# Columns of g2 summed late: one half among the last pieces of the output projection, the other between the first experts' weights

## The chip, the cores and the metric

The kernel runs on one core of a Trainium2 chip. The metric is the device time of one execution in microseconds. Engines are called PE (TensorE: matmuls, with its weight loads as PEld), DVE (VectorE), ACT (ScalarE), POOL (GpSimd) and SP (SyncE, which here only issues transfers).

## What is computed

One layer of a decoder trunk on 256 tokens of width 2048, in float32: a mixer of four kinds of attention with one input and one output projection, then a mixture of 16 experts. A vector c of the sequence gives six vectors by which the layer is modulated; g2, the last, scales the experts' output, column by column.

```python
mod = c_act @ ada_w[l] + ada_b[l]                      # c_act = silu(c); ada_w is 2048 x 12288
sh1, sc1, g1, sh2, sc2, g2 = jnp.split(mod, 6, axis=-1)
h = rmsnorm(x, norm1_g[l]) * (1.0 + sc1[:, None]) + sh1[:, None]
x = x + g1[:, None] * token_mixer(h, w_in[l], ..., w_out[l])
h = rmsnorm(x, norm2_g[l]) * (1.0 + sc2[:, None]) + sh2[:, None]
x = x + g2[:, None] * moe_ffn(h, router_w, router_bias, exp_w_gate[l], exp_w_up[l], exp_w_down[l])
return rmsnorm(x, final_g)
```

The reference computes all 16 experts for all tokens with a weight that is zero but for two; the kernel gathers, for each expert, up to 64 tokens (CAP) that chose it.

## The kernel before

**Stages.** Up to 146 us the sums for sc1 and sh1 run with the first pieces of the input projection; from 146 to 435 us the rest of the input projection, with the attention of the four mixers in between; then the output projection, to 547 us; the routing, to 557 us; then the experts in 8 pairs, and the last norm.

**The weight stream.** All weights come through one list of units in a fixed order, which SP issues (the class `Stream`). A unit is 128 partitions x 1024 float32 columns, 512 KB; a gate or up weight is a double unit of 1 MB (128x2048). Units wait in slots: a ring of 11 (names r, r_94 to r_98), and slots that are added when other data has been used up (ug, uo, uw, usc, ush among them; ugu is the name of a gate/up weight in such a slot, udh of a down weight). A slot takes its next unit when its last one has been read (`stream.done`); a unit can't pass the units ahead of it in the list. Two kinds of slot, for g2r and yhl, are used once and are added when all units ahead of the experts' have been issued.

**Projections.** A piece of w_in or w_out is one unit. `halves` splits it into a high part on ACT (whi, L584) and a low part on DVE (wlo, L586), in two buffers each (SPLITS = 2); then 24 matmuls read them (L561 to L563 with the weights moving or L565 to L567, names acc for the input and oacc for the output projection). In the output projection there are 32 pieces; each time that 512 columns of the result are complete, `add_part` multiplies them by g1 and adds them to x (L1190 and L1191 on DVE).

**The columns of the modulation.** g1 comes by matmuls, in 512-wide units between the pieces of the output projection (`akeys2`, from a list TAIL, at most 1.2 times the piece's number plus AHEAD). sc2, sh2 and g2 come on DVE: each in two blocks of 1024 columns, each block of 16 units. `ada_acc_v` multiplies the first unit by an element of c for each partition (L509) and adds the others in the same way, one operation for each (L511), to a running sum (ada_v). When a block is complete, `ada_cols` takes four matmuls with ones and a transpose (L520 to L523) to make columns of it (g2c). The units of the three stand among the pieces of the input projection (`akeys`, 96 units, evenly). `finish_cols` starts the last step of blocks whose sum is done.

**g2 as a row.** The experts' output has tokens in partitions, so g2 is needed as a row in all of them (g2r). `spread` makes 512 columns of it: four times a diagonal matrix of a column (dg, L533, DVE) and a matmul with ones (ada_r, L534), then a copy on ACT (L535). Before, the four calls stand in the loop over the first pair's eight weights, at n = 4 to 7. The first reader of g2r is the output of the first down projection (L1537).

**The routing.** After the last logits: a sum of squares (L1292), a root in steps of which one is on ACT (L1293, L405 to L414), the logits (L1305), then the choice of experts and the places of their tokens (to L1345).

**The experts.** For each pair p, `pair_units` lists 16 gate/up units (GUORDER: (c, g) for c = 0, 1, then 2 and 3, each for two experts) and 16 down units. The first pair's loop gathers the tokens (pg, L1410) as it goes, multiplies (gatep, upp, L201 and L204), and releases each weight behind its last matmul. The order on each engine is the order in which the program is recorded, changed by a scheduler that moves instructions forward where their operands allow.

Of the kernel before, what the change touches and what calls it, by code (L numbers as in the profile page):

```python
# [11 lines left out]
F32 = mybir.dt.float32  # L12
# [15 lines left out]
VEC = {(n, h) for n in ("sc2", "sh2", "g2") for h in range(2)}  # L28
TAIL = ("g1",)
NEG = -1e30  # L30
# [150 lines left out]
def hybrid_trunk_kernel(  # L181
# [59 lines left out]
    def wout_units(n):  # L241
# [10 lines left out]
        return [((("o", n), u), mk(u)) for u in range(8)]  # L252

    def pair_units(p):
        def mkg(c, g, e):
            return lambda t: nc.sync.dma_start(t, (gateT, upT)[g][:, c, 2 * p + e])
# [8 lines left out]
        def mkc(c):  # L265
            return lambda t: nc.sync.dma_start(
                t.rearrange("p (e f n) -> p e f n", e=2, f=4),
                downT[:, 2 * p:2 * p + 2, :, 1536 + 128 * c:1664 + 128 * c])
        us = [((("gu", p), c, g, e), mkg(c, g, e), 2) for c, g in GUORDER for e in range(2)]
        for h in range(2 if p < NP - 1 else 1):  # L270
            us += [((("dh", p, h), f, e), mkh(h, f, e)) for f in range(4) for e in range(2)]
# [13 lines left out]

    acol = {"sh1": 0, "sc1": 2048, "g1": 4096, "sh2": 6144, "sc2": 8192, "g2": 10240}

    def ada_tile(key):
        return ada_units(acol[key[0]] + 256 * key[1], key, 256, 4)

    def ada_block(key):
        nm, b, width = key
        return ada_units(acol[nm] + 512 * b, key, width, UNIT // width)

    def ada_blocks(nm):
        return [k for h in range(2) for k in ([(nm, 2 * h, 1024)] if (nm, h) in VEC else
                                              [(nm, 2 * h, 512), (nm, 2 * h + 1, 512)])]

    units = []
# [11 lines left out]
    wkeys = [u[0] for i in range(NEARLY, nw) for u in win_units(i)[3 * (i == SIXTH):]]  # L311
    blocks = [k for nm in ("sc2", "g1", "sh2", "g2") if nm not in TAIL for k in ada_blocks(nm)]
    lines = [[(k, u) for k in blocks if k[2] == width for u in range(KC * width // UNIT)] for width in (1024, 512)]
# [20 lines left out]
    order2, fi = [], 0  # L334
    akeys2 = [(k, u) for nm in TAIL for k in ada_blocks(nm) for u in range(KC * k[2] // UNIT)]
    for i in range(32):
        order2.append(("o",) + opieces[i])
        while fi < len(akeys2) and fi < 1.2 * i + AHEAD:
            order2.append(("a",) + akeys2[fi])
            fi += 1  # L340
    order2 += [("a",) + k for k in akeys2[fi:]]
    for it in order2:
# [693 lines left out]
    def run(gen):  # L1036
        for _ in gen:
            pass
# [50 lines left out]
    def finish_cols(age):  # L1089
        for c in late_cols:  # L1090
            c[0] += 1
        while late_cols and late_cols[0][0] > age:
            late_cols.pop(0)[1]()
# [331 lines left out]
    ssy = const.tile([128, 2, 7], F32, name="ssy")  # L1425
    fgr = []
    for p in range(NP):
        xg = xgs[p // 2]
        gp = ps("mm", [128, 512], name="gatep")
        up = ps("mm", [128, 512], name="upp")  # L1430
        for n, (c, g) in enumerate(GUORDER):
            if n == 5:
                weights(p)
            if p == 0 and n > 3:

                b = n - 4
                if b == 0:
                    g2r = late.tile([128, D], F32, name="g2r", tag="g2r")
                spread(g2c[:, 4 * b:4 * b + 4], g2r[:, 512 * b:512 * b + 512])
            o = (gp, up)[g]  # L1440
            keys = [(("gu", p), c, g, e) for e in range(2)]
            bt = Batch()
            for i in range(4):
# [5 lines left out]
                for e in (1, 0):  # L1449
                    w = stream.get(keys[e])[:, 512 * i:512 * i + 512]  # L1450
                    s0 = 2 * CAP * (p % 2) + CAP * e
                    bt(mm, o[64 * e:64 * e + 64, :], xg[:, k, s0:s0 + CAP], w, start=k == 0, stop=k == KC - 1)
            for key in keys:
                stream.done(key)
        run(first)
        if p == 0:
            yo2 = late.tile([128, 2, 512], F32, name="yo", tag="yo")
            yhl2 = late.tile([128, 2, 2, 512], F32R, name="yhl", tag="yhl")
# [214 lines left out]
```

## Time and profile before

| what | value |
|---|---|
| time, median of 3 | 1056.02 us (1053.86 to 1061.72) |
| the profiled execution | 1056.39 us, its span 1054.6 us |
| PE busy | 960.3 us, 91% |
| DVE busy | 500.4 us, 47% |
| ACT busy | 353.1 us, 33% |
| moved by DMA | 371.14 MB, mean 352 GB/s |
| chain that ended last, by engine | PE 66%, DMA 15%, DVE 8%, ACT 5%, issue 4% |

The profile is of one execution. The shares are means over stages that differ, so the rows below read it by stretches of time. PEclk is the share of TensorE's full clock that was granted. The DMA share is the mean busy share of 16 DMA engines; a share can read a little over 1. A duration in a row of the timeline is that of one instruction, or of as many as its count says, one behind the other; what stands in brackets is how long the engine stood idle before it, and whose end released it.

### The profile page before, as it was taken

Reading aid. Unit: us, or ns where it says so; the run is one execution under the profiler, and the core shown is the slowest. Engines: PE = TensorE matmul, PEld = TensorE weight load, DVE = VectorE, ACT = ScalarE, POOL = GpSimd, SP = SyncE. Lnnn points to the kernel's source line nnn. Section 1 sums busy time; section 2 is a strip of 40 time slices with the busy share of each in tenths; the row PEclk is TensorE's granted clock in tenths of the full one; section 3 lists DMA queues with packets and bytes.
Section 4 is the critical chain, followed back from the end, with each engine's and each line's share of the span. In section 5 each row is a group of like instructions: output and inputs, shape, how many; then the busy total and the mean of one; then the engine's idle time right before and its main releaser. Section 6 shows DMA issues by size and latency. Waiting matters only on the chain.

```text
span 1054.6 us, 16417 instructions
## 1 busy us (share of the span) xinstructions
PE 960.3 (91%) x6465; PEld 582.9 (55%) x6465; DVE 500.4 (47%) x1006; ACT 353.1 (33%) x763; POOL 4.8 (0%) x14
## 2 busy tenths in 40 slices
PE   5899999999999998989998999999889897899994
PEld 1677778898788985656784433433243232433323
DVE  2444566996998998344445231414024040422215
ACT  3333344566776768534444101100010000200013
POOL 0000000000000000000000000000000000000000
PEclk9999999999999999999998999999999999999998
DMA  9999999996999999889653999999999999999994
GB/s 332 357 358 359 357 323 325 355 373 210 335 325 348 325 384 387 307 270 384 228 214 145 341 421 414 412 417 415 422 407 421 412 420 413 419 419 414 421 359 128
DMA packets 153596, 371.14 MB, mean 352 GB/s; under 512 B 11514, under 2 KB 90275, under 8 KB 136875
## 3 DMA queue, kind: packets, MB, share of 16 engines
q1 hardware_dynamic: 152512, 368.41, 94.2%
q10 hardware_dynamic: 938, 1.61, 0.4%
q8 instruction: 53, 0.87, 0.3%
q14 instruction: 29, 0.23, 0.1%
q0 software_dynamic: 64, 0.02, 0.0%
HBM read 367.91 MB, written 2.10 MB: 351 GB/s over the span
## 4 chain that ended last, share of the span: by engine, by line
PE 66%; DMA 15%; DVE 8%; ACT 5%; issue 4%; SPq 0%; DVEq 0%; ACTq 0%
PE dn L201 10%; DMA ugu<-in_exp_w_up_dram 9%; PE acc L561 5%; PE acc L562 4%; PE acc L563 4%; PE gatep L201 4%; PE upp L201 3%; PE ada L201 3%; PE upp L204 3%; DMA r<-in_exp_w_up_dram 3%; PE oacc L565 3%; PE pg L1410 3%; PE oacc L566 3%; PE oacc L567 3%; PE gatep L204 2%
## 5 line engine op out<-in xcount | busy, mean ns | idle before, releaser
L561 PE MATMUL acc<-Hh,wlo 128*128 128x256 f32 x512 | 145.7, 294 | 6.3 <-DVE wlo L586 3.9
L562 PE MATMUL acc<-Hl,whi 128*128 128x256 f32 x512 | 146.1, 288 | 0.0
L563 PE MATMUL acc<-Hh,whi 128*128 128x256 f32 x512 | 145.2, 286 | 0.0
L586 DVE TENSOR_TENSOR wlo<-r,whi 128x1024 fp32r<-128x1024 f32 x85 | 103.8, 1221 | 62.7 <-ACT whi L584 60.1
L584 ACT CAST whi<-r 128x1024 fp32r<-128x1024 f32 x85 | 88.9, 1047 | 77.2 <-PE acc L563 28.7
L561 PEld LDWEIGHTS acc<-Hh,wlo 128*128 128x128 f32 x512 | 96.3, 192 | 16.9 <-DVE wlo L586 7.0
L562 PEld LDWEIGHTS acc<-Hl,whi 128*128 128x128 f32 x512 | 98.6, 193 | 3.5 <-issue 2.6
L563 PEld LDWEIGHTS acc<-Hh,whi 128*128 128x128 f32 x512 | 98.6, 193 | 2.7 <-issue 2.3
L511 DVE SCALAR_TENSOR_TENSOR ada_v<-r,cT,ada_v 128x1024 f32<-128x1024 f32 x75 | 95.9, 1279 | 0.4
L204 PE MATMUL upp<-ugu,xg 128*64 128x512 f32 x220 | 90.7, 597 | 4.4 <-DMA ugu<-in_exp_w_up_dram 4.4
L1464 DVE TENSOR_TENSOR he<-upp,sg 128x128 f32<-128x128 f32 x32 | 7.1, 282 | 180.0 <-PE upp L204 180.0
L204 PE MATMUL gatep<-ugu,xg 128*64 128x512 f32 x192 | 82.2, 601 | 0.5 <-DMA ugu<-in_exp_w_gate_dram 0.5
L1543 ACT CAST yhl<-yo 128x512 fp32r<-128x512 f32 x31 | 19.1, 618 | 164.1 <-DVE yo L1537 136.8
L204 PE MATMUL gatep<-r,xg 128*64 128x512 f32 x176 | 71.1, 596 | 0.9 <-DMA r<-in_exp_w_gate_dram 0.9
L201 PE MATMUL dn<-udh,heT 128*64 128x512 f32 x140 | 68.0, 599 | 1.0 <-DVE heT L1481 1.0
L1494 DVE TENSOR_TENSOR xt<-xt,sco 128x512 f32<-128x512 f32 (+1 forms) x70 | 42.1, 637 | 55.4 <-PE sco L1493 54.9
L204 PE MATMUL upp<-r,xg 128*64 128x512 f32 x148 | 65.7, 596 | 2.6 <-DMA r<-in_exp_w_up_dram 2.6
L204 PE MATMUL dn<-udh,heT 128*64 128x512 f32 x140 | 67.6, 599 | 0.0
L1460 ACT ACTIVATE sg<-gatep 128x512 f32<-128x512 f32 x8 | 4.8, 597 | 167.9 <-PE gatep L204 167.9
L565 PE MATMUL oacc<-wlo,Oh 128*128 128x512 f32 (+1 forms) x160 | 58.8, 369 | 0.2
L201 PE MATMUL dn<-r,heT 128*64 128x512 f32 (+1 forms) x124 | 55.5, 558 | 1.6 <-DVE heT L1481 1.6
L567 PE MATMUL oacc<-whi,Oh 128*128 128x512 f32 (+1 forms) x160 | 56.8, 355 | 0.0
(404 smaller groups left out, 1909.0 us busy)
## 6 DMA issues: line engine op xcount, KB each, us to landing
r<-in_ada_w_dram SPq DMA_DIRECT2D x156, 512.0 KB, 7.6
udh<-in_exp_w_down_dram SPq DMA_DIRECT2D x70, 512.0 KB, 11.4
r<-in_w_in_dram SPq DMA_DIRECT2D x69, 512.0 KB, 7.3
ugu<-in_exp_w_up_dram SPq DMA_DIRECT2D x34, 1024.0 KB, 14.6
ugu<-in_exp_w_gate_dram SPq DMA_DIRECT2D x33, 1024.0 KB, 13.8
r<-in_exp_w_gate_dram SPq DMA_DIRECT2D x31, 1024.0 KB, 13.0
r<-in_exp_w_up_dram SPq DMA_DIRECT2D x30, 1024.0 KB, 14.3
r<-in_exp_w_down_dram SPq DMA_DIRECT2D x56, 512.0 KB, 11.4
```

The lines of the kernel that those rows point to most:

```text
L201: ins = op(*args, **kw).ins
L204: ins = op(*args, **kw).ins
L511: V.scalar_tensor_tensor(acc, w, cT[:, u:u + 1], acc[:], OP.mult, OP.add)
L561: ins = mm(o, wl, hh, start=first, stop=False)
L562: mm(o, wh, hl, start=False, stop=False)
L563: mm(o, wh, hh, start=False, stop=last)
L565: ins = mm(o, hh, wl, start=first, stop=False)
L566: mm(o, hl, wh, start=False, stop=False)
L567: mm(o, hh, wh, start=False, stop=last)
L584: A.copy(hi, w)
L586: V.tensor_tensor(lo, w, hi[:].bitcast(F32), OP.subtract)
L1494: V.tensor_tensor(y(t, cs), y(t, cs), o, OP.add)
```

## The change

g2 leaves the list of the input projection, which then holds 64 units of sc2 and sh2. Its two blocks go to two places:

- Block 0's 16 units stand among pieces 18 to 31 of the output projection, behind each piece as many as G2FROM = 17 gives.
- Block 1's 16 units stand between the gate/up units of the first pair, from the seventh on (G2AT = 6), and `ada_item` sums each right behind the release of the weight ahead of it.
- `finish_cols(0)` comes at n = 4 of the first pair's loop, for block 0, and again behind the gather's last part, for block 1. Rows 0 and 1 of g2r are spread at n = 5 and 6, rows 2 and 3 behind the loop.
- The functions that list the units (`acol`, `ada_tile`, `ada_block`, `ada_blocks`) stand further up, unchanged.

```diff
 VEC = {(n, h) for n in ("sc2", "sh2", "g2") for h in range(2)}
-TAIL = ("g1",)
+TAIL = ("g1", "g2")
+G2FROM = 17
...
+    G2AT = 6
+    g2late = {n: [(ada_blocks("g2")[1], u) for u in range(KC) if G2AT + u * (16 - G2AT) // KC == n] for n in range(16)}
+
     def pair_units(p):
...
         us = [((("gu", p), c, g, e), mkg(c, g, e), 2) for c, g in GUORDER for e in range(2)]
+        if p == 0:
+            for n in range(len(us) - 1, G2AT - 1, -1):
+                us[n + 1:n + 1] = [ada_block(k)[u] for k, u in g2late[n]]
...
-    blocks = [k for nm in ("sc2", "g1", "sh2", "g2") if nm not in TAIL for k in ada_blocks(nm)]
+    blocks = [k for nm in ("sc2", "sh2") for k in ada_blocks(nm)]
...
-    akeys2 = [(k, u) for nm in TAIL for k in ada_blocks(nm) for u in range(KC * k[2] // UNIT)]
+    akeys2 = [(k, u) for k in ada_blocks("g1") for u in range(KC * k[2] // UNIT)]
+
+    g2keys = [[(k, u) for u in range(KC)] for k in ada_blocks("g2")]
+    gi = 0
     for i in range(32):
         order2.append(("o",) + opieces[i])
         while fi < len(akeys2) and fi < 1.2 * i + AHEAD:
             order2.append(("a",) + akeys2[fi])
             fi += 1
+        while gi < KC * (i - G2FROM) / (31 - G2FROM):
+            order2.append(("a",) + g2keys[0][gi])
+            gi += 1
...
+    def g2_row(b):
+
+        spread(g2c[:, 4 * b:4 * b + 4], g2r[:, 512 * b:512 * b + 512])
+
...
-            if p == 0 and n > 3:
-
-                b = n - 4
-                if b == 0:
-                    g2r = late.tile([128, D], F32, name="g2r", tag="g2r")
-                spread(g2c[:, 4 * b:4 * b + 4], g2r[:, 512 * b:512 * b + 512])
+            if p == 0 and n == 4:
+                finish_cols(0)
+                g2r = late.tile([128, D], F32, name="g2r", tag="g2r")
+            if p == 0 and n in (5, 6):
+                g2_row(n - 5)
...
-            for key in keys:
+            for e, key in enumerate(keys):
                 stream.done(key)
+                if p == 0:
+                    for it in g2late[2 * n + e]:
+                        ada_item(*it)
         run(first)
+        if p == 0:
+            finish_cols(0)
+            for b in (2, 3):
+                g2_row(b)
```

Lines move: L509 and L511 of before are L523 and L525 of the changed kernel, L586 is L600, L1190 and L1191 are L1204 and L1205, L256 and L259 (gate/up and down transfers) are L274 and L277, L219 (columns of the modulation) is L220.

On DVE, in the last third of the output projection, before (wlo is the split of a piece from the slot named, oacc the piece's sums, xt is x):

```order
L586 TENSOR_TENSOR wlo<-uo_5419,whi 128x1024
L586 TENSOR_TENSOR wlo<-r_95,whi 128x1024
L586 TENSOR_TENSOR wlo<-uo_5467,whi 128x1024 x2
L1190 TENSOR_TENSOR work<-oacc,g1b 128x512 x2
L1191 TENSOR_TENSOR xt<-xt,work 128x512 x2
L586 TENSOR_TENSOR wlo<-r_98,whi 128x1024 x2
```

and at the same place of the changed kernel (ada_v is the running sum of g2's block 0):

```order
L600 TENSOR_TENSOR wlo<-r_96,whi 128x1024
L525 SCALAR_TENSOR_TENSOR ada_v<-ug_5493,cT,ada_v 128x1024
L600 TENSOR_TENSOR wlo<-ug_5490,whi 128x1024
L525 SCALAR_TENSOR_TENSOR ada_v<-r_94,cT,ada_v 128x1024
L525 SCALAR_TENSOR_TENSOR ada_v<-ug_5521,cT,ada_v 128x1024
L600 TENSOR_TENSOR wlo<-ug_5493,whi 128x1024
L1204 TENSOR_TENSOR work<-oacc,g1b 128x512
L525 SCALAR_TENSOR_TENSOR ada_v<-r_96,cT,ada_v 128x1024
L1205 TENSOR_TENSOR xt<-xt,work 128x512
L1204 TENSOR_TENSOR work<-oacc,g1b 128x512
L525 SCALAR_TENSOR_TENSOR ada_v<-uo_5545,cT,ada_v 128x1024
L600 TENSOR_TENSOR wlo<-r_97,whi 128x1024
```

Between two splits there now stand one sum, or two, and two more among the operations that add a block to x.

On DVE, in the routing, from the sum of squares to the logits, before (v, rs_s, rs_r and rs_t are steps of the root, dg a diagonal for g2's row):

```order
L1292 TENSOR_REDUCE v_6011<-ss_4943 128x2
L533 TENSOR_SCALAR dg<-ident,g2c 128x128
L1293 TENSOR_SCALAR v_6011<-v_6011 128x2
L410 RECIPROCAL rs_r_6017<-rs_s_6015 128x2
L412 SCALAR_TENSOR_TENSOR rs_t_6019<-rs_r_6017 128x2
L413 TENSOR_TENSOR rs_t_6019<-rs_t_6019,v_6011 128x2
L414 SCALAR_TENSOR_TENSOR rs_6014<-rs_t_6019,rs_r_6017 128x2
L533 TENSOR_SCALAR dg<-ident,g2c 128x128
L1305 SCALAR_TENSOR_TENSOR logit<-lg,rs_6014,bsb 128x16 x2
```

and of the changed kernel, from the same sum of squares:

```order
L1306 TENSOR_REDUCE v_5967<-ss_4860 128x2
L523 TENSOR_SCALAR ada_v<-ug_5621,cT 128x1024
L547 TENSOR_SCALAR dg<-ident,g2c 128x128 x2
L1307 TENSOR_SCALAR v_5967<-v_5967 128x2
L525 SCALAR_TENSOR_TENSOR ada_v<-r_97,cT,ada_v 128x1024
L547 TENSOR_SCALAR dg<-ident,g2c 128x128
L424 RECIPROCAL rs_r_5973<-rs_s_5971 128x2
L547 TENSOR_SCALAR dg<-ident,g2c 128x128
L525 SCALAR_TENSOR_TENSOR ada_v<-ug_5882,cT,ada_v 128x1024
L426 SCALAR_TENSOR_TENSOR rs_t_5975<-rs_r_5973 128x2
L547 TENSOR_SCALAR dg<-ident,g2c 128x128 x2
L525 SCALAR_TENSOR_TENSOR ada_v<-r_95,cT,ada_v 128x1024
```

The first four sums of block 1 now stand between the steps of the root, and more of dg.

On SP, the last transfers of the first pair's gate and up weights, before (ugu and r are slots; L259 is the first down weight behind them):

```order
L256 DMA ugu_5662<-in_exp_w_gate_dram 128x2048
L256 DMA r_95<-in_exp_w_gate_dram 128x2048
L256 DMA ugu_5693<-in_exp_w_up_dram 128x2048
L256 DMA r_98<-in_exp_w_up_dram 128x2048
L256 DMA ugu_5824<-in_exp_w_gate_dram 128x2048
L256 DMA r_97<-in_exp_w_gate_dram 128x2048
L256 DMA ugu_5935<-in_exp_w_gate_dram 128x2048
L256 DMA ugu_6009<-in_exp_w_up_dram 128x2048
L256 DMA ugu_6007<-in_exp_w_gate_dram 128x2048
L256 DMA r_96<-in_exp_w_up_dram 128x2048
L256 DMA r_94<-in_exp_w_up_dram 128x2048
L259 DMA r_95<-in_exp_w_down_dram 128x1024
```

and of the changed kernel, up to the first weight whose slot the experts' matmuls free (the last row; in before those are the two up weights ahead of the last row):

```order
L274 DMA ugu_5847<-in_exp_w_gate_dram 128x2048
L274 DMA r_94<-in_exp_w_up_dram 128x2048
L220 DMA r_95<-in_ada_w_dram 128x1024
L274 DMA ugu_5964<-in_exp_w_gate_dram 128x2048
L220 DMA ug_6148<-in_ada_w_dram 128x1024
L274 DMA ugu_5961<-in_exp_w_gate_dram 128x2048
L220 DMA ug_6148<-in_ada_w_dram 128x1024
L220 DMA r_97<-in_ada_w_dram 128x1024
L220 DMA ug_6204<-in_ada_w_dram 128x1024
L220 DMA r_95<-in_ada_w_dram 128x1024 x2
L277 DMA r_97<-in_exp_w_down_dram 128x1024
L274 DMA ugu_6092<-in_exp_w_gate_dram 128x2048
```

Units of g2 (in_ada_w) now stand between the weights; four gate/up weights stand ahead of the 9 first rows of before, six ahead of those of the changed kernel, and the last four units of g2 behind its last row.

## Rows read from the trace of the kernel before

**Rows 1.** Windows: span; length, busy us by engine, PEclk, DMA share, GB/s
```profile
146.00:200.00 54.00, 50.36 (x506) 44.31 (x507) 41.96 (x75) 26.74 (x55) 1.05 (x2) 1.00 1.02 343
200.00:300.00 100.00, 96.72 (x795) 84.94 (x795) 83.91 (x163) 65.65 (x163) 0.00 (x0) 1.00 0.91 313
300.00:400.00 100.00, 96.37 (x780) 86.72 (x779) 92.66 (x158) 68.88 (x168) 0.00 (x0) 0.98 1.00 349
400.00:435.00 35.00, 31.12 (x175) 19.10 (x175) 21.20 (x57) 22.45 (x63) 0.00 (x0) 0.90 0.94 343
```

The engines in these rows stand in the order PE, PEld, DVE, ACT, POOL; in brackets the number of instructions.

**Rows 2.** The same windows, output projection and routing
```profile
435.00:475.00 40.00, 37.12 (x246) 22.78 (x245) 19.41 (x45) 18.75 (x39) 1.68 (x3) 0.96 0.89 294
475.00:505.00 30.00, 30.00 (x155) 19.29 (x154) 12.18 (x14) 13.24 (x23) 0.00 (x0) 1.00 1.06 383
505.00:547.00 42.00, 42.00 (x287) 37.40 (x286) 19.49 (x23) 16.82 (x25) 0.00 (x0) 1.00 0.55 202
547.00:557.00 10.00, 5.22 (x38) 4.16 (x36) 7.59 (x36) 8.13 (x17) 0.00 (x0) 0.79 0.62 234
```

**Rows 3.** The same windows, the experts
```profile
557.00:570.00 13.00, 12.92 (x54) 6.93 (x56) 8.48 (x18) 7.72 (x14) 0.00 (x0) 0.77 0.01 2
570.00:600.00 30.00, 30.00 (x152) 13.00 (x150) 8.48 (x20) 5.48 (x9) 0.00 (x0) 1.00 0.88 323
600.00:700.00 100.00, 95.94 (x460) 39.05 (x458) 30.84 (x60) 10.53 (x18) 0.00 (x0) 1.00 1.02 414
700.00:1020.00 320.00, 287.61 (x1288) 106.26 (x1286) 75.19 (x149) 27.09 (x46) 0.00 (x0) 1.00 1.02 415
```

**Rows 4.** The chain that ended last: start us, us, work
```profile
695.10 15.74 DMA ugu<-in_exp_w_up_dram
```

**Rows 5.** Tile ada_v: shortest, median, longest ns; and the page's DMA issues
```profile
L511 DVE SCALAR_TENSOR_TENSOR ada_v<-r,cT,ada_v x75: 1254/1279/1286, 150.5 to 409.4; 128x1024 f32<-128x1024 f32 x75
L509 DVE TENSOR_SCALAR ada_v<-r,cT x5: 744/752/753, 146.8 to 374.9; 128x1024 f32<-128x1024 f32 x5
...
r<-in_ada_w_dram SPq DMA_DIRECT2D x156, 512.0 KB, 7.6
```

**Rows 6.** PE's groups, 146 to 435 us: busy, mean ns, idle before, releasers
```profile
L561 PE MATMUL acc<-Hh,wlo 128*128 128x256 f32 x352 | 102.3, 294 | 6.2 <-DVE wlo L586 3.9 <-ACT Hh L627 2.1
L565 PE MATMUL acc<-wlo,Hh 128*128 128x256 f32 x128 | 37.5, 293 | 1.3 <-DVE wlo L586 1.3
L204 PE MATMUL PT<-ident,prob 128*128 128x128 f32 x110 | 17.5, 281 | 5.5 <-ACT prob L956 4.7 <-DVE ada_v L522 0.7
```

**Rows 7.** Timeline of the output projection, on ACT, DVE and PE: start us, us
```profile
518.61 1.05 ACT L584 CAST whi<-uo 128x1024 fp32r<-128x1024 f32 x1 [1.68 <-PE oacc L567]
519.69 1.23 DVE L586 TENSOR_TENSOR wlo<-uo,whi 128x1024 fp32r<-128x1024 f32 x1 [1.50 <-ACT whi L584]
520.84 1.28 DVE L1190 TENSOR_TENSOR work<-oacc,g1b 128x512 f32<-128x512 f32 x2
522.03 1.28 DVE L1191 TENSOR_TENSOR xt<-xt,work 128x512 f32<-128x512 f32 x2
523.24 1.22 DVE L586 TENSOR_TENSOR wlo<-r,whi 128x1024 fp32r<-128x1024 f32 x1
...
521.14 0.28 PE L565 MATMUL oacc<-wlo,Oh 128*128 128x256 f32 x1
```

**Rows 8.** Timeline of the routing, on DVE and on PE
```profile
549.76 0.28 DVE L533 TENSOR_SCALAR dg<-ident,g2c 128x128 f32<-128x128 f32 x1
550.39 0.17 DVE L410 RECIPROCAL rs_r<-rs_s 128x2 f32<-128x2 f32 x1 [0.27 <-ACT rs_s L405]
...
556.02 0.17 PE L1341 MATMUL rk<-sel,selb 128*128 128x16 bf16 x1 [3.45 <-DVE sel L1331]
```

**Rows 9.** Timeline on SP: two issues next to each other in its queue
```profile
551.06 0.33 SPq L256 DMA_DIRECT2D ugu<-in_exp_w_gate_dram  x1
570.83 0.33 SPq L256 DMA_DIRECT2D r<-in_exp_w_up_dram  x1
```

More of the change, by code (lines that the diff above doesn't have):

```diff
@@ L252, in wout_units, with ada_tile, ada_block, ada_blocks @@
         return [((("o", n), u), mk(u)) for u in range(8)]
+    acol = {"sh1": 0, "sc1": 2048, "g1": 4096, "sh2": 6144, "sc2": 8192, "g2": 10240}
+    def ada_tile(key):
+        return ada_units(acol[key[0]] + 256 * key[1], key, 256, 4)
+    def ada_block(key):
+        nm, b, width = key
+        return ada_units(acol[nm] + 512 * b, key, width, UNIT // width)
+    def ada_blocks(nm):
+        return [k for h in range(2) for k in ([(nm, 2 * h, 1024)] if (nm, h) in VEC else
+                                              [(nm, 2 * h, 512), (nm, 2 * h + 1, 512)])]
+    G2AT = 6
+    g2late = {n: [(ada_blocks("g2")[1], u) for u in range(KC) if G2AT + u * (16 - G2AT) // KC == n] for n in range(16)}
     def pair_units(p):
@@ L284, in early_unit @@
         return (("we", k), lambda t: nc.sync.dma_start(t, winT[:, k, 3840:4864]))
[L286 to L297, printed above, removed]
     units = []
```

## The prediction

> **What bounds the kernel now.** I read the windows by stage first, since the page's shares are means over stages with different limits. [rows 1] has the input projection with the attention (146 to 435 us), [rows 2] the output projection and the routing, [rows 3] the experts. From 146 to 435 us PE is busy 93 to 97% of the time, DVE up to 93%, the DMA engines 91 to 102%: three engines near their limit, with PE first. From 505 to 547 us PE is busy for all of 42.00 us, and DMA falls to a share of 0.55: the slots of the weight stream are full of expert weights that nobody reads yet. From 557 to 570 us it moves 2 GB/s for the same reason. From 600 us on the DMA share is 1.02 at 414 to 415 GB/s, and of 320 us PE works 287.61: there the bytes set the pace. The chain of waits says so too: one wait for an up weight is 15.74 us long [rows 4]. So time taken from PE's waits counts before 570 us, and bytes count after it. Then I read the sums that move [rows 5], what PE waits for in the input projection [rows 6], and three places in the timeline: the split of a w_out piece [rows 7], the routing [rows 8], and the issue of the first expert weights [rows 9].
>
> **What moves.** Two blocks of g2, 32 pieces of 512 KB [rows 5] (0.524 MB each, 16.8 MB), each summed on DVE: 2 × 0.752 + 30 × 1.279 = 39.9 us of DVE. No byte and no sum disappears. Block 0's 16 sums go among output pieces 18 to 31, block 1's between the gate/up weights of the first pair.
>
> **Term 1, the input projection gives back.** DVE loses 39.9 us of its 240 busy us from 146 to 435 (the four rows of [rows 1]), the stream 16.8 of some 97 MB. But PE's own work stays, so no more returns than what PE idles: 3.64 + 3.28 + 3.63 + 3.88 = 14.4 us, and the time lost to the lower granted clock in two rows, 0.02 × 100 + 0.10 × 35 = 5.5 us. Bounds 0 and 19.9. [rows 6] names PE's waits: for the low half of a split (wlo) 3.9 and 1.3 us, for a column sum's transpose 0.7, all on DVE; 4.7 for the softmax on ACT, which removed sums reach only indirectly. I take 60% of the idle time (8.7) and 2.3 of the clock: **−11**.
>
> **Term 2, the output projection takes 16 sums.** A piece goes through ACT's whi (1.05), DVE's wlo (1.23) and then PE's 24 matmuls; whi starts when PE releases the buffer [rows 7]. That wlo starts at 519.69 and ends at 520.92, PE takes it at 521.14: 0.22 us to spare. The next wlo may start 1.50 us after the one before ended (the idle time in its row). One sum of 1.28 fits; two (2.56) hold wlo for 1.06. In the changed order two sums stand between two splits twice, once together with the four operations that add a block to x, two of 0.64 behind 520.84 and two behind 522.03. I count three of these at 0.64 there: 1.06, then 1.92 + 2.56 − 1.50 = 2.98, and once more about 1.7: 5.8 us. Against it stands what PE does meanwhile (transposes and router matmuls, some 1.7), and that before has a stop of the same kind: the wlo at 523.24 follows x's last addition at once, and is 1 us later than its turn. I take **+3**; bounds 0 and 16 × 1.28 = 20.5, if no sum found a gap.
>
> A page of the Trainium skill speaks against the change here: "TensorE: Matmul & The Clock Gate", section "Architectural detail: the array is 16× 32×32, not 1× 128×128", says that the queues of ACT and DVE are strictly first in, first out, so a sum whose piece has not landed holds every split behind it. By that rule all 16 sums count whole where the pieces come late, and this term is 20 us instead of 3. The wlo at 523.24, which starts as the addition ahead of it ends, agrees with the order, though it waits for work, not for a transfer.
>
> **Term 3, the routing takes four sums.** In DVE's new order block 1's first sum (0.75) and three more (1.28 each) stand between the steps that lead to the root and the logits; together 4.6 us. DVE waits there only 0.27 us, for ACT's root [rows 8]. PE waits for this chain already (3.45 us for sel), so what DVE adds goes straight on to PE and all behind it. Four more operations on dg than before stand there too, 0.28 us each: 1.1. 4.6 + 1.1 − 0.3 = 5.4: **+5**. Bounds 0, if the pieces' sums slip into idle time that I don't see, and 7, if a sum also waits for its piece for some 2 us.
>
> **Term 4, the experts take the bytes.** The first slot that the experts free is that of the first gate/up weights, at 570.83 [rows 9]. By then before has issued 13 of 16 gate/up weights (1.049 MB each) and one down weight; its queue in SP's rows shows this, with the ninth of the last nine at 551.06. By SP's new order, after has issued 10 of them, one down weight, block 0 and 12 pieces of block 1; the other four stand behind a gate weight that must wait for that slot. So 3 × 1.049 + 4 × 0.524 = 5.24 MB more remain for the stage that is bound by bytes: at 415 GB/s 12.6 us. From 570 to 600 before moves only 323 GB/s [rows 3]; the new transfers can fill up to 30 us × 92 GB/s = 2.8 MB of it, 6.7 us. Bounds 5.9 and 12.6; far bound, if none of block 1 has moved by then, 8.4 MB = 20.2 us. I take **+8**. PE's additions here (8 matmuls on columns and 16 that spread rows, 3 us) and DVE's 12 sums hide in what PE waits for bytes, 32 us of 320; without that cover they would cost 3 us.
>
> The Trainium skill, "DMA: Bandwidth & Descriptors", section "Specifications", gives a core's share of HBM as some 358 GB/s. By it 5.24 MB would take 14.6 us (an estimate from that page); the trace differs, 414 to 415 GB/s in this stage, and the measurement decides.
>
> **Sum.** −11 + 3 + 5 + 8 = +5. The profiled execution took 1056.4 us (span 1054.6), 0.4 us over the median of 1056.02: **1061 us**.
>
> **Rivals.**
> R1, faster: the split chain on DVE, not PE, paces the input projection, and the sums moved lie in gaps. For it: DVE at 92.66 of 100 us from 300 to 400, and wlo as the largest wait. Against it: PE is busy for 96.37 of the same 100 us. Then term 1 is −19.9, terms 2 and 3 are 0 and 1, and term 4 is 8: −11, 1045 us. It decides from a gain of 19 us in that stage, with the late sums hidden.
> R2, slower: the second half's bytes are paid whole in the experts. All 16 pieces wait behind the routing, since DVE doesn't consume them there and their slots stay taken: 8.4 MB / 415 = 20.2 us instead of 8, so 1073 us. For it: 1.02 of DMA share until 1020 us, nothing hides a byte there. Against it: DMA moves 2 GB/s from 557 to 570, room for 5 MB if slots come free. It decides when over 7 MB more than before remain at the first slot.
> R3, slower: sums hold the splits in the output projection, as in term 2's upper bound; 20.5 instead of 3 is 1078 us, half of the 16 exposed 1068. For it: 0.22 us to spare, PE 42.00 of 42 busy. Against it: most gaps hold one sum, and DVE is busy there for 19.49 of 42 us only.
> R4, no gain: PE's waits go to the softmax instead (term 1 at −3): 1069 us, for which only the 4.7 us on prob speak; counted with R2's chance.
>
> **How the numbers follow.** The forecast (all terms within their bounds, sum between −10 and +10): 0.47. R1: 0.18. R2 with R4: 0.22. R3: 0.13. About 1%, 10.5 us, is what a measurement can tell from no change: faster is under 1045.5, slower over 1066.6. So faster 0.18, same 0.47, slower 0.35. The range reaches down to R1's 1045 and up to 1077, past R2 and short of R3's end; what lies outside is the tail of R1 and of R3, 2 in 10. The forecast's own range is 1051 to 1066.
>
> **What the changed profile would show.** Term 1: the experts' gather minus the time that terms 2 and 3 added starts 11 us earlier; PE over 97% busy up to 435. Term 2: PE's idle time between output pieces 23 and 28, at wlo (L600 there), about 3 us. Term 3: sel or the logits 5 us later behind the last output piece, with ada_v rows between the root and logit. Term 4: from the first gather to the end 8 us more, at the same 415 GB/s, with the 4 late pieces between gate weights. The prediction is wrong if DMA from 570 to 600 fills up and the experts' stage is no longer (then 1053), or if PE's idle time in the input projection stays at 14 us (1072).

## The result, and the profile after

The changed kernel took 1066.31 us, the kernel before 1056.02 us, both medians of 11 runs (the table ahead of the prediction has 3); the ratio is 1.0094, 95% interval 1.0074 to 1.0114. One of the changed kernel's runs took 2423.41 us at a mean granted clock of 0.40, and the ratio leaves it out. So the kernel became slower by 0.9%: inside the range (1045 to 1077) and, by 0.3 us, inside the 1% that was called no change (up to 1066.6), but 0.3 us above the forecast's own 1051 to 1066; the predicted time was 1061. On another chip the changed kernel took 1067.40 beside 1057.30 us, ratio 1.0095 (1.0064 to 1.0126).

The windows by stage of the changed kernel; the columns are those of [rows 1], and the rows answer to [rows 1 to 3]:

```profile
146.00:200.00 54.00, 50.28 (x496) 44.94 (x496) 33.99 (x58) 25.65 (x47) 1.06 (x2) 0.97 0.92 300
200.00:300.00 100.00, 95.05 (x756) 82.27 (x757) 72.16 (x151) 66.95 (x169) 0.00 (x0) 0.97 0.77 248
300.00:400.00 100.00, 97.62 (x801) 85.98 (x801) 80.99 (x157) 71.62 (x176) 0.00 (x0) 1.00 0.98 338
400.00:435.00 35.00, 34.93 (x232) 24.32 (x231) 20.93 (x64) 28.12 (x79) 0.00 (x0) 1.00 0.73 242
435.00:475.00 40.00, 39.15 (x242) 26.87 (x241) 21.40 (x36) 16.52 (x23) 1.68 (x3) 1.00 0.77 257
...
505.00:547.00 42.00, 38.31 (x281) 33.50 (x280) 33.11 (x48) 16.47 (x30) 0.00 (x0) 0.99 1.00 383
...
557.00:570.00 13.00, 12.11 (x48) 4.86 (x48) 7.84 (x14) 5.03 (x9) 0.00 (x0) 0.77 0.26 82
570.00:600.00 30.00, 28.74 (x154) 13.72 (x152) 21.56 (x32) 5.04 (x9) 0.00 (x0) 1.00 0.87 342
...
700.00:1020.00 320.00, 289.83 (x1301) 108.10 (x1298) 76.52 (x149) 25.22 (x43) 0.00 (x0) 0.98 1.02 415
```

DVE and DMA are lighter up to 435 us (DVE 208.07 us instead of 239.73 over the four rows, DMA 248 instead of 313 GB/s in the second). The bytes have gone to 505 to 547 us, 383 instead of 202 GB/s, and behind it. From 700 us on the pace is the same 415 GB/s.

Four events cut the execution into the stages that the terms speak of: the last output matmul, the first matmul of the gather, the first gate matmul, and PE's last matmul. PE's timeline, before:

```profile
547.44 0.28 PE L567 MATMUL oacc<-whi,Oh 128*128 128x256 f32 x1
...
557.08 1.19 PE L1410 MATMUL pg<-oh,xh 128*128 128x256 f32 x4 [0.83 <-DVE oh L1379]
...
561.22 1.12 PE L201 MATMUL gatep<-ugu,xg 128*64 128x512 f32 x1
...
1040.41 1.36 PE L1490 MATMUL sco<-yo,M 128*128 128x128 f32 x6 [0.53 <-DVE xt L1494]
```

and of the changed kernel:

```profile
540.37 0.28 PE L581 MATMUL oacc<-whi,Oh 128*128 128x256 f32 x1
...
554.05 1.19 PE L1424 MATMUL pg<-oh,xh 128*128 128x256 f32 x4 [0.84 <-DVE oh L1393]
...
559.17 1.11 PE L202 MATMUL gatep<-ugu,xg 128*64 128x512 f32 x1 [0.89 <-DVE xg L1431]
...
1052.63 0.71 PE L1515 MATMUL sco<-yo,M 128*128 128x128 f32 x4 [0.18 <-DVE xt L1519]
```

| stage | before | after | difference | predicted |
|---|---|---|---|---|
| to the last output matmul (terms 1 and 2) | 547.44 | 540.37 | −7.1 | −8 |
| from there to the first gate matmul (term 3) | 13.78 | 18.80 | +5.0 | +5 |
| from there to the end on PE (term 4) | 480.55 | 494.17 | +13.6 | +8 |
| sum | 1041.77 | 1053.34 | +11.6 | +5 |

The end on PE is its last start plus duration, 1040.41 + 1.36 and 1052.63 + 0.71. So terms 1 and 2 together, and term 3, came out within 1 us of what was predicted, and the experts cost 5.6 us more than I took. Whether the first three came out for the reasons given is a question of its own, taken up further down.

### The profile page after: what moved, and what is told of

Same layout as the page of the kernel before. It is cut to its first block, busy times and chain, and to the rows that moved or that the text cites. A ratio compares the mean times of both kernels' runs of the same rounds, so it can differ in the third digit from the quotient of the medians.

```text
span 1066.5 us, 16398 instructions
## 1 busy us (share of the span) xinstructions
PE 966.5 (91%) x6465; PEld 585.6 (55%) x6465; DVE 503.9 (47%) x1006; ACT 355.6 (33%) x765; POOL 4.8 (0%) x14
## 4 chain that ended last, share of the span: by engine, by line
PE 60%; DMA 25%; DVE 9%; ACT 3%; issue 2%; SPq 0%; DVEq 0%; ACTq 0%
PE dn L202 8%; DMA ugu<-in_exp_w_up_dram 6%; DMA ugu<-in_exp_w_gate_dram 5%; PE acc L575 5%; PE acc L576 4%; PE acc L577 4%; DMA r<-in_ada_w_dram 4%; PE ada L202 3%; PE upp L202 3%; PE gatep L202 3%; PE upp L205 3%; DMA r<-in_exp_w_gate_dram 3%; PE pg L1424 3%; PE oacc L579 2%; PE oacc L580 2%
## 5 line engine op out<-in xcount | busy, mean ns | idle before, releaser
L600 DVE TENSOR_TENSOR wlo<-r,whi 128x1024 fp32r<-128x1024 f32 x91 | 111.2, 1223 | 87.5 <-ACT whi L598 87.0
L598 ACT CAST whi<-r 128x1024 fp32r<-128x1024 f32 x91 | 95.1, 1046 | 84.1 <-PE acc L577 26.7
L205 PE MATMUL upp<-ugu,xg 128*64 128x512 f32 x220 | 95.8, 600 | 1.3 <-DMA ugu<-in_exp_w_up_dram 1.3
L205 PE MATMUL gatep<-ugu,xg 128*64 128x512 f32 x184 | 89.1, 622 | 0.0
L205 PE MATMUL gatep<-r,xg 128*64 128x512 f32 x184 | 85.3, 605 | 0.5 <-DMA r<-in_exp_w_gate_dram 0.5
L525 DVE SCALAR_TENSOR_TENSOR ada_v<-r,cT,ada_v 128x1024 f32<-128x1024 f32 x61 | 78.2, 1281 | 5.5 <-DMA r<-in_ada_w_dram 5.1
L205 PE MATMUL upp<-r,xg 128*64 128x512 f32 x148 | 70.8, 594 | 0.0
L205 PE MATMUL dn<-udh,heT 128*64 128x512 f32 x132 | 64.8, 600 | 0.0
L202 PE MATMUL dn<-udh,heT 128*64 128x512 f32 x128 | 61.9, 598 | 1.6 <-DVE heT L1506 1.6
L202 PE MATMUL dn<-r,heT 128*64 128x512 f32 x116 | 56.6, 599 | 1.0 <-DVE heT L1506 1.0
L205 PE MATMUL dn<-r,heT 128*64 128x512 f32 x112 | 55.9, 598 | 0.0
## 6 DMA issues: line engine op xcount, KB each, us to landing
udh<-in_exp_w_down_dram SPq DMA_DIRECT2D x65, 512.0 KB, 11.4
r<-in_exp_w_gate_dram SPq DMA_DIRECT2D x29, 1024.0 KB, 13.5
r<-in_exp_w_down_dram SPq DMA_DIRECT2D x57, 512.0 KB, 11.4
r<-in_exp_w_up_dram SPq DMA_DIRECT2D x28, 1024.0 KB, 12.7
```

What stands on the lines that cost most here:

```text
L202: ins = op(*args, **kw).ins
L205: ins = op(*args, **kw).ins
L525: V.scalar_tensor_tensor(acc, w, cT[:, u:u + 1], acc[:], OP.mult, OP.add)
L598: A.copy(hi, w)
L600: V.tensor_tensor(lo, w, hi[:].bitcast(F32), OP.subtract)
```

## The experiments

All ran on a chip beside the kernel before; times are medians. Stage times come from PE's timeline of each run's profile, as above. One thing limits what they can tell: up to the end of the output projection, executions of one program differ by some us. The changed kernel's two profiles have the last output matmul at 540.37 and 541.94 us, and two runs whose program is the same up to there (the second and the fourth below) at 537.14 and 537.39. The experts' stage repeats better: 494.2 and 493.3 us in the changed kernel's two profiles.

**Nothing of g2 at all.** Edit: no units of it in any list, its columns set to one.

```diff
-    g2late = {n: [(ada_blocks("g2")[1], u) for u in range(KC) if ...] for n in range(16)}
+    g2late = {n: [] for n in range(16)}
...
-        while gi < KC * (i - G2FROM) / (31 - G2FROM):
-            order2.append(("a",) + g2keys[0][gi])
-            gi += 1
...
+    V.memset(g2c, 1.0)
```

> The change with g2 left out (no transfers and no sums of it, its columns set to one): what the input projection and the output projection take without it, and the experts with as many weights ahead as before. Theory: input projection and output projection -8 to -9 with nothing given back: 1047 to 1048 us. Rival (DVE and DMA pace the input projection more than PE, the late sums took back most of it): 1040 us or less.

Measured: 1047.45 us, ratio 0.9916 (0.9891 to 0.9941). The last output matmul starts here:

```profile
536.85 0.28 PE L579 MATMUL oacc<-whi,Oh 128*128 128x256 f32 x1
```

536.85 − 547.44 = −10.6: this is term 1 alone, in one profile each, predicted −11; by the times the whole kernel gained 0.84%, about 9 us. The experts take 480.7 us, as before (480.55). R1, that DVE paces the input projection and 19 us or more come back there, falls.

**Block 1's sums behind the routing.**

```diff
-                    for it in g2late[2 * n + e]:
-                        ada_item(*it)
+                    with tc.issue_after(placed):
+                        for it in g2late[2 * n + e]:
+                            ada_item(*it)
```

> The change with block 1's sums held behind the choice of the experts, so that none stands between the steps of the root and the logits. Theory: the routing gives back 4 to 5 us (last output piece to first gather 13.7 us in the change, 9.6 before); the slots that those four sums held come free later, one down weight and one piece of g2 fewer stand ahead of the first blocked transfer, 1.0 MB more are left, +2.5: 1064 us. Rival (the sums in the routing were waiting time anyway): the routing stays at 13 us and the time at 1066 us or more.

Measured: 1063.95 us, ratio 1.0079 (1.0051 to 1.0107). The interval overlaps that of the change, so the time alone doesn't tell them apart; the stage does. From the last output matmul to the first of the gather it takes 9.77 us instead of 13.68 (before 9.64):

```profile
537.14 0.28 PE L581 MATMUL oacc<-whi,Oh 128*128 128x256 f32 x1
...
546.91 1.19 PE L1424 MATMUL pg<-oh,xh 128*128 128x256 f32 x4 [0.83 <-ACT xh L1381]
```

The experts take 493.5 us, nearly what they take in the change (494.2), though 1.1 MB more are left when their first slot comes free (196.0 instead of 194.9 MB, summed from the packets of the traces), as expected; 44 us after the first gate matmul the two are equal (183.3 MB).

**Block 1's sums without its transfers.** As the run above, and the sums read columns of x (`xt[:, 0, 0:1024]`) in place of 16 units that are no longer listed.

> As the run with block 1's sums behind the routing, but block 1's 16 transfers are left out: its sums read columns of x that are resident instead, so half of g2 is not what it should be. Sums, their matmuls and the spread of g2 stay in the experts' stage. Theory (bytes): 12 gate/up and 2 down weights ahead of the first blocked transfer, 0.5 MB more than before instead of 6.3, so 13 to 14 us less than that run: about 1050 us. Rival (DVE's sums and the late matmuls among the experts' own work cost the time): within 4 us of that run.

Measured: 1052.95 us, ratio 0.9973 (0.9953 to 0.9993): 11.0 us less than with the transfers, 13 to 14 expected. Sums, columns and rows of g2 stood in the experts' stage all the same, so the bytes cost most of what the stage had grown by. It took 485.5 us, 8.0 less than with them, still 4.9 more than before; these 4.9 are not explained (see the end of the next section).

**Block 1's transfers without its sums.**

```diff
         w = stream.get((key, u))
+        if key[0] == "g2" and key[1] == 2 and u < KC - 1:
+            stream.done((key, u))
+            return None
```

> The change with block 1's transfers kept, but 15 of its 16 sums left out (half of g2 is not what it should be); the slots are released unread. Theory: the routing gives back 4 to 5 us; the slots come free as soon as a piece has landed, so all 16 pieces, 10 gate/up and 5 down weights stand ahead of the first blocked transfer, 1.0 MB more than before instead of 5.2, -10: about 1051 us. Rival (8.4 MB can't be hidden anywhere, slots or not): only the routing's part, 1061 us.

Measured: 1057.17 us, ratio 1.0006 (0.9986 to 1.0027), 9.1 us less than the change, where I expected 15 and the rival 5. The experts' stage fell by 4.7 us only (489.5), so part of the bytes stayed unhidden even though no sum held their slots. The expectation had counted all 16 pieces ahead of the first blocked transfer; in SP's queue four of them still stand behind a gate weight that waits, and 3.1 MB more than before are left when the first slot comes free, not 1.0.

**One block late.** Block 0 late and block 1 back in the input projection (e1), and the reverse (e2):

```diff
-    blocks = [k for nm in ("sc2", "sh2") for k in ada_blocks(nm)]
+    blocks = [k for nm in ("sc2", "sh2") for k in ada_blocks(nm)] + ada_blocks("g2")[1:]
```

(for e2 `[:1]`), with the other list of late units emptied.

> Block 0 of g2 late among the output pieces, as in the change; block 1 back among the input projection's pieces. Theory (bytes left at the first freed slot set the experts' time): SP's order here has 12 gate/up weights and 2 down weights ahead of the first transfer that waits for the experts' matmuls, before 13 and 1, so 0.5 MB more are left, 1.3 us; the input projection gives back half of what it did, -4; the output projection costs +1, the routing nothing: 1054 to 1055 us. Rival (the late sums in the output projection hold the splits): 1060 us or more.

> Block 1 of g2 late between the first experts' weights, as in the change; block 0 back among the input projection's pieces. Theory (bytes): 10 gate/up weights, 2 down weights and about 12 pieces of block 1 stand ahead of the first transfer that waits for the experts' matmuls, so 4.7 MB more than before are left, 11 us; -4 in the input projection, +2 in the routing for two sums in its chain: 1064 to 1067 us, all of the change's loss. Rival (the loss comes from both halves alike): 1060 us.

Measured: 1070.37 us, ratio 1.0133 (1.0098 to 1.0168), and 1080.62 us, ratio 1.0242 (1.0207 to 1.0278). Both are misses, by 15 us, and slower than with both blocks late. Of the loss 10.6 and 7.5 us lie before the last output matmul, which starts at 558.06 and 554.94 us; the rest lies in the experts (486.6 and 487.5 us) and, in e2 as in the change, in the routing (13.65 us). With 96 sums in the input projection it is 547.44, with 64 it is 537 to 542, with 80 it is later than with either. In e1 and e2 alike PE's longest wait there is one of 5.45 us for vc, values of mixer D's compression (a step of its attention that shortens keys and values); this is e1's:

```profile
205.85 1.08 PE L897 MATMUL pcTp<-ident,pc 128*128 128x128 f32 x4 [5.45 <-DVE vc L857]
```

The kernel before has no such wait; the change has 3.32 us of it (shown below). From 146 to 300 us PE idles 12.7 us in e1 and 9.7 in e2, at a granted clock of 0.94 and 0.97; before it was 6.9 us at 1.00.

**Both blocks among the output pieces.**

```diff
-        while gi < KC * (i - G2FROM) / (31 - G2FROM):
-            order2.append(("a",) + g2keys[0][gi])
+        while gi < min(32, 32 * (i + 1) / 30):
+            order2.append(("a",) + (g2keys[0] + g2keys[1])[gi])
```

> Both blocks among the output pieces, about one sum behind each of the 32 pieces; nothing of g2 between the experts' weights. Theory (bytes): 13 gate/up weights stand ahead of the first blocked transfer as before, so the experts cost nothing more if the transfers keep up; -8 in the input projection, +2 in the output projection: 1050 us. Rival (sums hold the splits in the output projection, or its transfers come late, as 16.8 MB more must pass in some 112 us that moved 32 MB): 1060 us or more, with waits for pieces on DVE or PE.

Measured: 1057.27 us, ratio 1.0003 (0.9987 to 1.0019), between theory and rival: the experts take 483.1 us, 11 less than in the change, but the last output matmul starts at 546.74, 9.9 us later than without g2. The rival's second reason shows: from 475 us on PE idles 6.8 us, 2.21 and 1.12 of it in waits for pieces of g1 that come through the same list (DMA uo), at a DMA share of 1.04.

**The transfers of w1 earlier.** The changed kernel with `W1AT = (0, 2)` in place of `(1, 3)`: the transfers of w1, the weights of mixer D's compression, stand one place earlier in the list. Beside it ran the change itself on the same chip.

> The change with the transfers of w1 (the compression of mixer D) one place earlier in the list: behind the first and the third piece, not the second and the fourth. In the change's trace PE waits 3.32 us at 199 us for the copies vc, since the order on PE has no piece between the compression's last matmuls and the transposes that need its outcome (before: 73 matmuls of pieces); here 126 stand there. Theory (the wait moved there by the change eats part of what the input projection gives back): this wait and the drop of the granted clock around it go (0.91 from 180 to 220 us), 4 to 7 us less than the change: 1059 to 1062 us. Rival (the idle time only moves to a later chain): within 2 us of the change.

> The changed kernel once more, for a comparison on one chip with the two runs beside it: 1066 us.

Measured: 1062.60 us, ratio 1.0041 (1.0018 to 1.0063), beside 1067.40 us, ratio 1.0095 (1.0064 to 1.0126): 4.8 us less. The wait that it was made for looks like this in the change, on DVE and then on PE:

```profile
198.62 1.29 DVE L525 SCALAR_TENSOR_TENSOR ada_v<-r,cT,ada_v 128x1024 f32<-128x1024 f32 x1 [0.31 <-DMA r<-in_ada_w_dram]
...
200.93 1.18 DVE L857 COPY vc<-vcp 15x128 f32<-15x128 f32 x4
...
202.26 1.08 PE L897 MATMUL pcTp<-ident,pc 128*128 128x128 f32 x4 [3.32 <-DVE vc L857]
```

It is gone in the new run, but PE's idle time from 146 us to the last output matmul is no shorter (12.7 us, 12.1 in the change's second profile), in smaller waits, most of them for wlo, of 1.1 to 1.8 us: as the rival had it. What did come back is the granted clock: 1.00 instead of 0.97 from 146 to 200 us and 0.98 instead of 0.97 from 200 to 300, an estimated 0.03 × 54 + 0.01 × 100 = 2.6 us. So the time agrees with the theory, and its reason only in part.

**Wider, and ahead of the tail.** 12 units of g2 in the input projection and 20 among the output pieces, none among the experts: the 12 behind its last 12 pieces (e9), or ahead of these with all the other sums (e11). Two more things differ from the change in both: the rate is raised by which the sums of sc2 and sh2 are listed, so that these are done 12 pieces earlier, and w1 stands earlier (`W1AT = (0, 1)` in e9, `(0, 2)` in e11).

```diff
+        if n >= len(wkeys) - 12:
+            order.append(("a",) + g2all[n - len(wkeys) + 12])
```

(e9; e11 has `akeys += g2all[:12]` instead.)

> g2's 32 units spread wider: the first 12 behind the last 12 pieces of the input projection, 20 among the output pieces, none among the experts; the transfers of w1 behind the first two pieces. 13 gate/up weights stand ahead of the first blocked transfer as before. Theory: from 380 to 460 us DMA has a share of 0.7 to 0.85 in the runs without g2 there, room for 12 pieces, so that the output projection's transfers no longer set its pace as in the run with both blocks there; input projection -8, output projection +2, experts 0: 1048 to 1052 us. Rival (every sum put back into the input projection costs what its removal gave): 1056 us or more.

> As the run with g2's units spread wider, but the 12 early units stand with the other sums ahead of the last 12 pieces of the input projection, where no sum stands now; 20 among the output pieces, none among the experts; the transfers of w1 behind the first and the third piece. Theory (a sum costs most where the attention's last chains run on DVE and PE has no piece left to cover them: from 403 to 468 us PE idled 16 us in the run with 12 sums there): those waits shrink to some 3 us as in the change, and the experts take as long as before: 1050 to 1054 us. Rival (it is the number of sums ahead of the output projection that counts, not their place): 1060 us or more.

Measured: 1063.81 us, ratio 1.0065 (1.0041 to 1.0089), and 1085.64 us, ratio 1.0272 (1.0246 to 1.0297). Both are misses, for the rivals. In e9 the experts take 480.7 us as expected, but the last output matmul starts at 554.75; in e11 at 571.34. My reason for e11 was wrong: with no sum behind the last 12 pieces the waits at the attention's end did not go. PE there:

```profile
469.23 0.68 PE L1044 MATMUL rr<-dg,ones 128*128 128x128 f32 x4 [2.09 <-DVE dg L1043]
472.38 0.67 PE L456 MATMUL perm<-A2n,ident 128*32 128x4 f32 x32 [2.47 <-DVE oT L1047]
476.31 0.67 PE L456 MATMUL perm<-B2n,ident 128*32 128x4 f32 x32 [3.27 <-DVE A L458]
479.34 0.61 PE L1188 MATMUL bb<-wbs,ones 128*128 128x16 f32 x2 [2.35 <-DVE B L458]
482.80 1.07 PE L205 MATMUL ada<-uo,cB 128*32 128x512 f32 x2 [2.86 <-DMA uo<-in_ada_w_dram]
```

13 us of idle in 16, in a chain between PE and DVE (and one transfer) that no matmul of a piece covers. In e9 the same five waits make 13.2 us. Since three things changed at once in these two runs, they don't tell which of them brought the chain there uncovered.

**Both effects together.** Both blocks among the output pieces, and `W1AT = (0, 2)`.

> Both blocks of g2 among the output pieces as in the earlier run with both there, and the transfers of w1 one place earlier. Theory: the two effects add, 1057 less the 4 to 5 us that the w1 place gave in the change: 1052 to 1053 us, below the kernel before. Rival (the output projection's transfers set its pace, at 390 GB/s up to the routing, so what is won ahead of it is waited for there): 1057 us.

Measured: 1053.07 us beside 1056.83, ratio 0.9962 (0.9942 to 0.9981): 13 us below the change, and below the kernel before by 0.4%, which is small but outside the interval. The last output matmul starts at 542.97, the routing takes 9.65 us, the experts 483.1.

## Why the prediction held, and where it was off

**Term 1** was right in size (−10.6 measured without g2, −11 predicted), and mostly wrong in its reason. PE's idle time from 146 to 435 us fell only from 14.4 to 3.72 + 4.95 + 2.38 + 0.07 = 11.1 us, where the term took back 8.7; the granted clock gave about 5.5 − (0.03 × 54 + 0.03 × 100) = 0.9 us, where it took 2.3. That is 4.2 us of 11, and PE is busy 96% there, not the over 97% that was to be the sign. Nor did the waits go that were named. In the changed kernel PE's groups from 146 to 435 us, beside [rows 6], read

```profile
L575 PE MATMUL acc<-Hh,wlo 128*128 128x256 f32 x352 | 102.6, 295 | 6.4 <-DVE wlo L600 4.1 <-ACT Hh L641 2.1
...
L897 PE MATMUL pcTp<-ident,pc 128*128 128x128 f32 x4 | 1.1, 427 | 3.3 <-DVE vc L857 3.3
```

The waits for wlo shrank from 3.9 + 1.3 to 4.1 us. What went are the softmax's 4.7 us, which the prediction took to be reached only indirectly. Most of them are one wait of the kernel before:

```profile
420.77 0.48 PE L204 MATMUL PT<-ident,prob 128*128 128x128 f32 x1 [3.52 <-ACT prob L956]
```

In its row, 400 to 435 us, PE idled 3.88 us (it was busy 89% there, not the 93 to 97% that the prediction read for all four rows), and now 0.07. In their place came 3.32 us for vc: in PE's order 73 matmuls stood before between the compression's last matmuls and the transposes that need them, most of them matmuls of pieces, and none after the change. I priced what the removed sums free, and not what else the new order on PE puts side by side. The rest of the gain lies from 435 to 475 us: PE idles 0.85 us instead of 2.88, at a granted clock of 1.00 instead of 0.96, an estimated 2.0 + 1.6 = 3.6 us. With the 1.1 us of term 2 against it, 4.2 + 3.6 − 1.1 = 6.7 of the change's 7.1 us are found. So the size of term 1 was in good part luck. R4, no gain since PE's waits go to the softmax instead, falls: those are the waits that went.

**Term 2**, +3, can't be told from the stage's length: against 536.85 us without g2, the same program gives 537.14, 537.39, 540.37 and 541.94. PE's waits tell it better: from 475 us to the last output matmul PE doesn't idle before, and idles 1.1 us in the changed kernel, in one stop that stands in all four profiles. DVE, then PE:

```profile
514.36 1.28 DVE L525 SCALAR_TENSOR_TENSOR ada_v<-uo,cT,ada_v 128x1024 f32<-128x1024 f32 x1
515.55 1.22 DVE L600 TENSOR_TENSOR wlo<-r,whi 128x1024 fp32r<-128x1024 f32 x1
...
516.82 0.39 PE L579 MATMUL oacc<-wlo,Oh 128*128 128x256 f32 x1 [1.06 <-DVE wlo L600]
```

The split starts right behind a sum, and PE idles 1.06 us. It stands among the operations that add a block to x, where the prediction had counted 2.98 or 1.7 us; the 1.06 that was worked out, for two sums in a row between two splits, cost nothing visible. So term 2 was about 2 us too high. R3, 16 exposed sums or half of them, falls. The 20 us that the prediction named for pieces that come late fall with it: from 475 us to the last output matmul none of DVE's idle times over 0.15 us ends with a transfer, so no sum held a split by waiting for its piece.

**Term 3** was right in its reason, and by a little luck in its size. In DVE's timeline the steps from the sum of squares to the logits take 548.79 − 542.45 = 6.3 us where they took 551.46 − 549.70 = 1.8. Before, and then of the changed kernel:

```profile
549.70 0.15 DVE L1292 TENSOR_REDUCE v<-ss 128x2 f32<-128x10 f32 x1
...
551.46 0.37 DVE L1305 SCALAR_TENSOR_TENSOR logit<-lg,rs,bsb 128x16 f32<-128x16 f32 x2
```

```profile
542.45 0.15 DVE L1306 TENSOR_REDUCE v<-ss 128x2 f32<-128x10 f32 x1
542.52 0.74 DVE L523 TENSOR_SCALAR ada_v<-ug,cT 128x1024 f32<-128x1024 f32 x1
...
543.64 1.28 DVE L525 SCALAR_TENSOR_TENSOR ada_v<-r,cT,ada_v 128x1024 f32<-128x1024 f32 x1
...
545.29 1.28 DVE L525 SCALAR_TENSOR_TENSOR ada_v<-ug,cT,ada_v 128x1024 f32<-128x1024 f32 x1
...
546.95 1.28 DVE L525 SCALAR_TENSOR_TENSOR ada_v<-r,cT,ada_v 128x1024 f32<-128x1024 f32 x1
...
548.79 0.38 DVE L1319 SCALAR_TENSOR_TENSOR logit<-lg,rs,bsb 128x16 f32<-128x16 f32 x2
```

Four sums, none of which waited for its piece: 4.6 us, as worked out; the 1.1 us taken for more operations on dg don't show. To the gather's first matmul the stage grew by 4.0 us (13.68 instead of 9.64). The last 1.0 us of the 5.0 lies behind it, and the prediction had not counted it: a fifth sum stands ahead of xg, for which PE's first gate matmul waits 0.89 us (its row is shown with PE's timeline).

```profile
557.24 1.31 DVE L525 SCALAR_TENSOR_TENSOR ada_v<-r,cT,ada_v 128x1024 f32<-128x1024 f32 x1
...
558.54 0.57 DVE L1431 TENSOR_SCALAR xg<-pg,A,B 128x256 f32<-128x256 f32 x1
```

The Trainium skill ("TensorE: Matmul & The Clock Gate", section "Architectural detail: the array is 16× 32×32, not 1× 128×128") says that DVE's queue is strictly first in, first out; the rows of the routing agree, since the small steps stand behind sums that nothing in the routing needs. Held behind the routing, the sums gave 3.9 us back.

**Term 4** is the step that failed, by its size. The bytes were counted rightly, the reclaimed part was not. What had moved 44 us after the first gate matmul, in the windows from 0 of before, of the change, of the run without block 1's transfers, and of the best run:

```profile
0.00:605.00 605.00, 560.75 (x4609) 429.17 (x4611) 378.34 (x761) 306.76 (x674) 4.78 (x14) 0.98 0.93 319
```

```profile
0.00:603.00 603.00, 558.92 (x4595) 428.91 (x4597) 380.13 (x755) 309.36 (x676) 4.78 (x14) 0.97 0.91 311
```

```profile
0.00:599.00 599.00, 562.50 (x4607) 429.39 (x4609) 380.35 (x757) 308.31 (x674) 4.79 (x14) 0.98 0.90 309
```

```profile
0.00:601.00 601.00, 558.18 (x4613) 428.12 (x4615) 380.27 (x761) 305.61 (x673) 4.79 (x14) 0.98 0.93 322
```

605 × 319 GB/s = 193.0 MB before, 603 × 311 = 187.5 MB after: 5.5 MB more are left. These rates are rounded; summed over the packets of the traces it is 5.3 MB, 12.7 us at 415 GB/s. The stage grew by 13.6 us, and by 12.7 in the change's second profile (493.26 us). The prediction's 5.24 MB at the first freed slot were right to the last digit (189.66 MB are left there before, 194.90 after), and nothing of it was won back in the 30 us behind: from 570 to 600 us DMA moved 342 instead of 323 GB/s, 0.6 MB more, in a stage that began 2 us earlier, where I had taken up to 2.8 and priced the term at 8. SP's queue there, of the changed kernel and then before:

```profile
569.79 0.33 SPq L274 DMA_DIRECT2D ugu<-in_exp_w_gate_dram  x1
570.21 0.86 SPq L220 DMA_DIRECT2D ug<-in_ada_w_dram  x2
...
578.31 0.81 SPq L220 DMA_DIRECT2D ug<-in_ada_w_dram  x2
579.21 0.38 SPq L274 DMA_DIRECT2D r<-in_exp_w_gate_dram  x1
```

```profile
570.83 0.81 SPq L256 DMA_DIRECT2D r<-in_exp_w_up_dram  x2
574.70 4.73 SPq L259 DMA_DIRECT2D r<-in_exp_w_down_dram  x3
```

Two of the four late pieces go out behind the gate weight at once, some 0.4 us each; the third waits for its slot until 578.31, and the next gate weight stands behind it. In the same time the queue of before issues two up weights and, from 574.70 us on, down weights. Whether the gate weight's own slot was free earlier isn't shown, so that the late pieces held it up is an argument, not a measurement. The upper bound, 12.6, was the better value: 1.0 short in one profile, 0.1 in the other. With 185.1 + 8.4 MB that were left out, and with 601 × 322 = 193.5 MB, the runs with no late bytes are at the level of before, and their stages are shorter: 485.5 and 483.1 us. In the other runs with late bytes the count is less exact. The table has, against the kernel before, what more is left when the experts free their first slot and 44 us after the first gate matmul (summed from the packets), what it costs at 415 GB/s, and how much longer the stage is:

| run | MB at the first slot | us | MB 44 us after the gate | us | stage longer, us |
|---|---|---|---|---|---|
| the change | 5.2 | 12.6 | 5.3 | 12.7 | 13.6 |
| e3, sums behind the routing | 6.3 | 15.2 | 5.2 | 12.5 | 13.0 |
| e8, w1 earlier | 5.4 | 12.9 | 4.1 | 9.8 | 13.5 |
| e5, transfers without sums | 3.1 | 7.6 | 2.5 | 6.1 | 9.0 |
| e2, block 1 late | 4.7 | 11.4 | 2.8 | 6.8 | 7.0 |

R2 (the second half's bytes paid whole, 20 us) falls by its own condition, over 7 MB more at the first slot; but what did remain was paid whole, as R2 had it, and 13.6 us lies about halfway between its 20 and the 8 of the forecast.

**What stays open.** Runs with as many bytes moved at that point as before (within 0.7 MB) still differ in the experts' stage: 480.7 without g2 and in e9, 483.1 in e7 and e12, 485.5 to 486.6 in e1, e4 and e11. In the last three 12 gate/up and 2 down weights stand ahead of the first blocked transfer, in the others 13 and 1; whether this order costs the 2 to 6 us wasn't tried. Nor is it settled why sums put back into the input projection, 12 or 16 of them, cost more than all 32 did in the kernel before. The runs show where PE waits, and it isn't one place: at the compression, before 300 us, in e1 and e2, and at the attention's end in e9 and e11, whose w1 and rate were changed too. They don't show what in the new order brings these chains there uncovered; e1 and e2 with w1 earlier weren't run.

## What to carry to other kernels

Where a stage is bound by bytes, count what is still to be moved when its first buffer comes free: here this difference over the measured rate, 12.6 us, came within 1 us of the loss in the changed kernel's two profiles; in other runs it was up to 4.4 us off (table above). A gap that seems free to take it up should be counted as zero until it is known that the queue's order lets transfers into it. An operation moved late in an in-order queue costs in full where the path that it now stands in has no idle time: four sums in the routing, 4.6 us. And where a scheduler orders the instructions, the gain of taking work out needn't be proportional: here half of the change was slower than none and than all of it. So price the new order, not only the work: a wait that was covered by other matmuls can come to stand alone.

## What was not expected

- The clock and the compression: with the wait for vc the granted clock was 0.97 from 146 to 300 us, and the place of two pairs of transfers (w1) changed the kernel by 4.8 us.
- Which waits went: those for the softmax on ACT, though all the work that was moved stood on DVE.
- How well the experts' stage repeats: 480.55, 480.67 and 480.72 us in three different kernels with the same weights ahead (before, e9 and e6), at 410 to 416 GB/s from 700 to 1020 us in all runs, while the end of the output projection moves by 5 us with the program the same.
